# A two-block transformer kernel: attention probabilities of the second block turned by the vector engine and by small DMAs

## The chip, the cores and the metric

The kernel runs on one core of a Trainium2 chip. TensorE (PE in the rows) multiplies matrices, with its weight loads shown apart as PEld; VectorE (DVE) and ScalarE (ACT) work on elements; GpSimd (POOL) does a few masks; SyncE (SP) issues most DMAs. The metric is the device time of one execution in microseconds (us), as the median over runs.

## The reference

A sequence of 512 tokens of width 1024 passes two blocks in float32. The change lies in the second one. What is computed around it, cut to the core:

```python
h = rms_norm_2(x, norm_g)
proj = h @ w_in                      # u, g_rnn, q, k, v, g_attn, m_rnn, m_attn
u = causal_depthwise_conv_2(u, conv_w, conv_b)
y_rnn = rg_lru(u, ...) * silu(g_rnn)
# sliding window attention: 16 query heads, 4 key/value heads, blocks of 128 queries,
# keys of the block before and of the own block, one sink per head
scores = einsum("bnqkgd,bnjkd->bnkgqj", qb, kw) / sqrt(64)
scores = where(valid, scores, -inf)
m = maximum(max(scores, -1), sink)
p = exp(scores - m)
probs = p / (sum(p, -1) + exp(sink - m))
out = einsum("bnkgqj,bnjkd->bnqkgd", probs, vw)
y_attn = rope'd attention out * silu(g_attn)
merged = sigmoid(m_rnn) * (y_rnn @ w_rnn_out) + sigmoid(m_attn) * (y_attn @ w_attn_out)
x = x + merged @ w_o
```

The probabilities come with queries on the partitions; the product with the values needs keys on the partitions, so each 128x128 square of probabilities has to be transposed.

## The kernel before

**Weights.** All weights lie in DRAM as 216 chunks of 128x1024 float32, eight 128x128 tiles each, in the order of use. `w_load` (L153) brings a chunk into one of two `raw` buffers through SP's queue. `w_split` makes two fp32r halves of it: ACT casts the high half `wh` (L169), DVE subtracts for the low half `wl` (L170). There are three buffers of each. `take` walks through the chunks: at the first tile of chunk c it splits c to c+2 and loads up to c+4. A load waits until the split two chunks earlier has freed its buffer, and a cast until TensorE has finished with a chunk three earlier.

**Projections.** `project` multiplies activations by eight tiles, three matmuls of 128x512 for each (L293 to L295: high by high, high by low, low by high). Its weights are the stationary operand's stream, so one chunk is 24 matmuls. After every fourth tile it calls `tick`.

**Background work.** Attention runs in pieces between the matmuls of the projections. A unit is a Python generator; `yield cost, delay` ends a piece, takes its cost from a credit that each tick raises by `rate`, and holds the unit for `delay` ticks. Two units of lane "a" are open at a time. `finish` runs what is left of a unit without ticks. On top of this order of writing, a scheduler sets the final order of each engine by its own estimate of when data are ready; each engine then works strictly in that order. So instructions of one unit can stand late in one engine's row and early in another's.

**The second attention.** `window_attention(kvp, n)` (L940) is one unit: one pair of key/value heads, one block of 128 queries; there are 8 units, called unit 1 to 8 below (kvp 0 with n 0 to 3, then kvp 1). For each e of the pair it makes the scores of four query heads into PSUM (L955, L956), masks them into a 128x512 tile `p` (L960 for n = 0, else an ACT copy L962 and a DVE copy under a mask L963), takes the maximum (L965), exponentials with sums (L972) and normalises (L978). Then TensorE transposes the four squares into a PSUM bank by a matmul with the identity (L986, 8 a unit, 64 in all). ACT copies the bank to SBUF as `own` (L987), DVE multiplies it by a mask as `prev` for n > 0 (L990; 12 in all). Four matmuls (two for n = 0) make the output (L1000) and DVE multiplies it by the gate (L1004).

**What runs beside it.** After units 1 to 4 are queued, the gate projections run, then for m = 0 to 8 the recurrent branch (`lru`, convolution, scan), then `br` 0 (yr: the recurrent output, split for TensorE by L286 on ACT and L289 on DVE, times `w_rnn_out_2`), then `br` 1, which needs all units (`finish(*units)`, L1087) and splits `ya` in the same way.

Of the kernel before, what the change touches and what calls it, by code (L numbers as in the profile page):

```python
# [14 lines left out]
P = 128  # L15
# [111 lines left out]
def tile_hybrid_two_block(ctx, tc, xT, wts, prm_d, row_d, sgw_d, rope_d, sink_d, out):  # L127
    nc = tc.nc
# [49 lines left out]
    def take(n, width=P):  # L178

        res = []  # L180
        for _ in range(n * P // width):
            c, o = divmod(wpos[0], CH)
            if o == 0 or not res:
                for cc in range(c, c + 3):
                    w_split(cc)
                for cc in range(c, c + 5):
                    w_load(cc)
            h, l = conv[c]
            res.append((h[:, o * P : o * P + width], l[:, o * P : o * P + width]))
            wpos[0] += width // P  # L190
        return res

    lanes, clk = {"a": [], "b": []}, {"t": 0, "credit": 0.0, "rate": 1.0, "a": 2, "b": 1}

    def add_bg(gen, lane="a"):
        task = [gen, 0, lane]
# [55 lines left out]
    class Area:  # L254
# [10 lines left out]
        def tmp(self, dt=F32):  # L265
            return self.tile([P, T], dt)
# [673 lines left out]
    def window_attention(kvp, n):  # L940
        nk = P if n == 0 else 2 * P
        qs = slice(n * P, (n + 1) * P)
        ks = slice((n + 1) * P - nk, (n + 1) * P)
        prs = []
        for e in range(2):
            kv = 2 * kvp + e
            S4 = area[0].tile([P, 4, P], F32, "p")
            prs.append(S4)
            m4, nm4, es, sm = (area[0].tile([P, 4], F32, "s") for _ in range(4))
            per = T // nk  # L950
            for j0 in range(0, 4, per):
                ps = bank("aux")
                for d in range(per):
                    z, q = ps[:, d * nk : (d + 1) * nk], QS[kv][:, j0 + d, qs]
                    PE.matmul(z, lhsT=q, rhs=KS[kvp][:, 2 * e, ks], start=True, stop=False)  # L955
                    PE.matmul(z, lhsT=q, rhs=KS[kvp][:, 2 * e + 1, ks], start=False, stop=True)  # L956
                z = ps.rearrange("p (d k) -> p d k", d=per)
                x = S4[:, j0 : j0 + per]
                if n == 0:
                    V.tensor_tensor(out=x, in0=z, in1=mask[:, 0:1].to_broadcast([P, 4, P]), op=ALU.add)  # L960
                else:
                    A.copy(out=x, in_=z[:, :, P:nk])  # L962
                    V.copy_predicated(x, mask[:, 1:2].bitcast(mybir.dt.int32).to_broadcast([P, 2, P]), z[:, :, 0:P])  # L963
                yield 0.5, 0
            V.tensor_reduce(out=m4, in_=S4, axis=mybir.AxisListType.X, op=ALU.max)  # L965
            sk = sink[:, kv * 4 : kv * 4 + 4]
            V.scalar_tensor_tensor(out=m4, in0=m4, scalar=0.125, in1=sk, op0=ALU.mult, op1=ALU.max)
            V.tensor_scalar(out=nm4, in0=m4, scalar1=-1.0, scalar2=None, op0=ALU.mult)  # L968
            V.tensor_tensor(out=es, in0=sk, in1=m4, op=ALU.subtract)
            A.activation(es, es, AF.Exp)  # L970
            for j in range(4):
                A.activation(  # L972
                    S4[:, j], S4[:, j], AF.Exp, scale=0.125, bias=nm4[:, j : j + 1], accum_out=sm[:, j : j + 1]
                )
            yield 0.95, 1
            V.tensor_tensor(out=sm, in0=sm, in1=es, op=ALU.add)
            V.reciprocal(out=sm, in_=sm)
            V.tensor_tensor(out=S4, in0=S4, in1=sm.unsqueeze(2).to_broadcast([P, 4, P]), op=ALU.mult)  # L978
            yield 0.9, e


        own, prev = [tmp(), tmp()], []
        for e in range(2):
            ps = bank("aux")
            for j in range(4):
                PE.transpose(ps[:, j * P : (j + 1) * P], prs[e][:, j], ident)  # L986
            A.copy(out=own[e], in_=ps)  # L987
            if n > 0:
                prev.append(tmp())
                V.tensor_tensor(  # L990
                    out=prev[e].rearrange("p (a b) -> p a b", a=4), in0=ps.rearrange("p (a b) -> p a b", a=4),
                    in1=mask[:, 2:3].to_broadcast([P, 4, P]), op=ALU.mult,
                )
        yield 1.4 if n else 0.1, 2
        po = bank("aux")
        sums = [(VV[:, n], own)] + ([(VD[:, n - 1], prev)] if n else [])
        for i, (v, w) in enumerate(sums):
            for e in range(2):
                f = kvp * P + e * 64
                PE.matmul(  # L1000
                    po[e * 64 : e * 64 + 64], lhsT=v[:, f : f + 64], rhs=w[e], start=i == 0, stop=i == len(sums) - 1
                )
        y = ya[kvp][:, :, qs]
        V.scalar_tensor_tensor(  # L1004
            out=y, in0=po.rearrange("p (a b) -> p a b", a=4), scalar=0.5, in1=y, op0=ALU.mult, op1=ALU.mult
        )
        yield 0.66, 5
# [11 lines left out]
            high_low(f, lo, hi, QS[2 * kvp][:, j])  # L1019
            high_low(f, hi, lo, QS[2 * kvp + 1][:, j])  # L1020
    finish(norm_task)
    clk.update(rate=1.05)
    units = []
    for kvp in range(2):
        ya.append(grp(F32))
# [176 lines left out]
```

## Time and profile before

| what | us |
|---|---|
| median of 3 runs | 1285.73 (1285.55 to 1285.8) |
| profiled execution, its own time | 1285.55 |
| its span, first to last instruction | 1283.8 |
| TensorE busy | 1272.5 |
| VectorE busy | 870.3 |
| ScalarE busy | 599.4 |

The span is what the profile shows of an execution; 1.75 us of the profiled execution lie outside it. Busy time is the time in which an engine has at least one instruction in work. Matmuls overlap: a 128x512 matmul lasts 390 ns in the rows, and the next starts some 227 ns after it, so the cost of a matmul in a row of matmuls is the distance of two starts, not its length. The same holds for DVE and ACT on a smaller scale. The granted TensorE clock is 0.998 of full speed over the whole span, which is the 2.4 GHz level.

### The profile page before, as it was taken

Reading aid. Unit: us, or ns where it says so; the run is one execution under the profiler, and the core shown is the slowest. Engines: PE = TensorE matmul, PEld = TensorE weight load, DVE = VectorE, ACT = ScalarE, POOL = GpSimd, SP = SyncE. Lnnn points to the kernel's source line nnn. Section 1 sums busy time; section 2 is a strip of 40 time slices with the busy share of each in tenths; the row PEclk is TensorE's granted clock in tenths of the full one; section 3 lists DMA queues with packets and bytes.
Section 4 is the critical chain, followed back from the end, with each engine's and each line's share of the span. In section 5 each row is a group of like instructions: output and inputs, shape, how many; then the busy total and the mean of one; then the engine's idle time right before and its main releaser. Section 6 shows DMA issues by size and latency. Waiting matters only on the chain.

```text
span 1283.8 us, 15409 instructions
## 1 busy us (share of the span) xinstructions
PE 1272.5 (99%) x5890; PEld 1033.8 (81%) x5890; DVE 870.3 (68%) x1313; ACT 599.4 (47%) x964; POOL 45.8 (4%) x85
## 2 busy tenths in 40 slices
PE   9999999999999999999999999999999999999997
PEld 7888787778788888888888888888878777788886
DVE  6899998776447697666664333897678896633355
ACT  6733555546323464444443222554558875532232
POOL 0100004320000000000000000000000000000000
PEclk9999999999999999999999999999999999999999
DMA  6332322112333423333333333324222222223341
GB/s 212 131 99 83 99 83 82 60 56 83 99 107 120 134 77 106 98 99 99 99 99 103 116 109 110 105 84 130 69 84 96 81 82 66 82 83 99 132 131 66
DMA packets 39114, 126.80 MB, mean 99 GB/s; under 512 B 4480, under 2 KB 6656, under 8 KB 39040
## 3 DMA queue, kind: packets, MB, share of 16 engines
q1 hardware_dynamic: 37808, 124.76, 30.7%
q8 instruction: 46, 0.75, 0.2%
q10 hardware_dynamic: 1232, 1.05, 0.2%
q14 instruction: 28, 0.23, 0.1%
HBM read 121.60 MB, written 4.19 MB: 98 GB/s over the span
## 4 chain that ended last, share of the span: by engine, by line
PE 95%; DVE 3%; ACT 1%; issue 1%; POOL 0%; DVEq 0%; ACTq 0%
PE mm L293 29%; PE mm L294 29%; PE mm L295 29%; PE aux L1000 1%; PE aux L638 1%; PE aux L293 1%; PE aux L295 1%; PE aux L294 1%; PE aux L669 1%; PE aux L986 1%; PE aux L955 1%; PE aux L682 1%; PE aux L956 1%; DVE t L1137 0%; PE aux L520 0%
## 5 line engine op out<-in xcount | busy, mean ns | idle before, releaser
L293 PE MATMUL mm<-g,wh 128*128 128x512 f32 x1592 | 623.7, 392 | 0.0
L294 PE MATMUL mm<-g,wh 128*128 128x512 f32 x1592 | 620.9, 390 | 0.4 <-DVE g L289 0.4
L295 PE MATMUL mm<-g,wl 128*128 128x512 f32 x1592 | 620.7, 390 | 0.0
L170 DVE TENSOR_TENSOR wl<-raw,wh 128x1024 fp32r<-128x1024 f32 (+1 forms) x212 | 258.1, 1218 | 212.8 <-ACT wh L169 210.0
L169 ACT CAST wh<-raw 128x1024 fp32r<-128x1024 f32 (+1 forms) x211 | 221.5, 1050 | 370.0 <-PE mm L294 267.2
L293 PEld LDWEIGHTS mm<-g,wh 128*128 128x128 f32 x1592 | 299.0, 188 | 67.0 <-issue 5.3
L295 PEld LDWEIGHTS mm<-g,wl 128*128 128x128 f32 x1592 | 299.0, 188 | 62.9 <-issue 0.3
L294 PEld LDWEIGHTS mm<-g,wh 128*128 128x128 f32 x1592 | 299.1, 188 | 61.5 <-DVE g L289 1.1
L490 DVE SCALAR_TENSOR_TENSOR g<-g,prm,g 128x505 f32<-128x505 f32 (+28 forms) x120 | 82.6, 742 | 0.8
L286 ACT CAST g<-t 128x512 fp32r<-128x512 f32 x46 | 28.1, 620 | 64.8 <-DVE t L822 54.3
L809 DVE SCALAR_TENSOR_TENSOR t<-mm,prm,t 128x511 f32<-128x511 f32 x72 | 53.7, 746 | 1.3
L289 DVE TENSOR_TENSOR g<-t,g 128x512 fp32r<-128x512 f32 x46 | 31.8, 698 | 14.3 <-ACT g L286 14.1
L286 ACT CAST g<-g 128x512 fp32r<-128x512 f32 x44 | 25.9, 619 | 23.7 <-DVE g L760 14.2
L972 ACT ACTIVATE p<-p,s 128x128 f32<-128x128 f32 x64 | 24.9, 390 | 19.1 <-DVE s L968 19.1
L820 ACT ACTIVATE t<-t 128x512 f32<-128x512 f32 x22 | 13.9, 632 | 40.4 <-DVE t L809 40.4
L656 DVE TENSOR_TENSOR_SCAN t<-t,zero 128x512 f32<-128x512 f32 (+3 forms) x32 | 27.1, 850 | 7.5 <-POOL t L651 7.3
L289 DVE TENSOR_TENSOR g<-g,g 128x512 fp32r<-128x512 f32 x44 | 29.2, 689 | 2.6 <-ACT g L286 2.1
L807 ACT ACTIVATE t<-mm,prm 128x512 f32<-128x512 f32 x36 | 27.9, 774 | 0.0
L376 ACT ACTIVATE t<-g 128x512 f32<-128x512 f32 (+1 forms) x29 | 17.1, 591 | 20.5 <-DVE g L1116 16.9
L356 ACT ACTIVATE g<-g,prm 128x512 fp32r<-128x512 f32 x24 | 17.2, 717 | 18.0 <-DVE g L768 16.9
L1098 DVE SCALAR_TENSOR_TENSOR t<-t,mm 128x512 f32<-128x512 f32 x8 | 5.5, 689 | 27.1 <-PE mm L295 27.1
L651 POOL TENSOR_SCALAR_AFFINE_SELECT t<-t 128x128 f32<-128x128 f32 x32 | 17.4, 544 | 146.1 <-ACT t L647 146.0
(265 smaller groups left out, 1205.0 us busy)
## 6 DMA issues: line engine op xcount, KB each, us to landing
raw<-in_wts SPq DMA_DIRECT2D x215, 512.0 KB, 3.6
g<-in_xT SPq DMA_DIRECT2D x8, 256.0 KB, 5.8
t<-in_xT SPq DMA_DIRECT2D x8, 256.0 KB, 3.7
spill<-g SPq DMA_DIRECT2D x8, 256.0 KB, 3.2
g<-spill SPq DMA_DIRECT2D x8, 256.0 KB, 4.1
out<-t ACTq DMA_DIRECT2D x4, 256.0 KB, 2.3
out<-t SPq DMA_DIRECT2D x4, 256.0 KB, 2.4
g<-in_row SPq DMA_DIRECT2D x1, 768.0 KB, 6.5
```

What stands on the lines that cost most here:

```text
L169: A.copy(out=h[:, o : o + step], in_=raw[c][:, o : o + step])
L170: V.tensor_tensor(out=l[:, o : o + step], in0=raw[c][:, o : o + step], in1=h[:, o : o + step].bitcast(F32), op=ALU.subtract,)
L286: A.copy(out=h, in_=src)
L289: V.tensor_tensor(out=l, in0=src, in1=h.bitcast(F32), op=ALU.subtract)
L293: PE.matmul(ps, lhsT=lh, rhs=rh, start=start, stop=False)
L294: PE.matmul(ps, lhsT=lh, rhs=rl, start=False, stop=False)
L295: PE.matmul(ps, lhsT=ll, rhs=rh, start=False, stop=stop)
L490: V.scalar_tensor_tensor(out=a[:, d:T], in0=c[:, 0 : T - d], scalar=pr("cv_w", (30 - d) * 4 + i), in1=a[:, d:T], op0=ALU.mult, op1=ALU.add,)
L656: V.tensor_tensor_scan(out=R[:, 0:cx][:, ::-1], data0=F[:, 0:cx][:, ::-1], data1=zero.to_broadcast([P, cx]), initial=1.0, op0=ALU.mult, op ...
L807: A.activation(a, y, AF.Identity, scale=pr("ffn_conv_w", 88 + m), bias=pr("ffn_conv_b", m))
L809: V.scalar_tensor_tensor(out=a[:, d:T], in0=y[:, 0 : T - d], scalar=pr("ffn_conv_w", (2 - d) * 44 + m), in1=a[:, d:T], op0=ALU.mult, op1=A ...
L972: A.activation(S4[:, j], S4[:, j], AF.Exp, scale=0.125, bias=nm4[:, j : j + 1], accum_out=sm[:, j : j + 1])
```

## The change

The four squares are no longer transposed on TensorE. DVE turns each 32x32 square of `p` in place of position (STREAM_TRANSPOSE, 128x512, one an e, 16 in all), into a tile `turned`. The squares then have to change places: ACT copies the four diagonal squares' strips into the new tile `w` (32 partitions by 4x32 each, 64 copies in all), and the twelve others go by DMA from SBUF to SBUF on SP's queue (32 partitions, 4 runs of 32 elements each: 16 KB a DMA, 192 DMAs in all), issued three at a time by `move()`. `prev` is now made from `w` in SBUF. For n = 0, where there is no `prev`, DVE copies 128x4 elements of `w` onto themselves. The order of the two halves of the output's sum is reversed, delays and costs of the yields change, and from the second block's gate projections on, `take` loads up to c+3 instead of c+4.

```diff
-                for cc in range(c, c + 5):
+                for cc in range(c, c + clk["ahead"]):
                     w_load(cc)
...
+        own, moves = [], []
+        cuts = [slice(32 * i, 32 * i + 32) for i in range(4)]
+        def move():
+            for o, i in moves.pop(0) if moves else ():
+                nc.sync.dma_start(out=o, in_=i)
...
-                yield 0.5, 0
+                move()
+                yield 0.5, 1
...
+            move()
             yield 0.95, 1
...
-            yield 0.9, e
-        own, prev = [tmp(), tmp()], []
+            yield 0.7, 0
+            turned, w = tmp(), tmp()
+            V.transpose(out=turned, in_=S4.rearrange("p a b -> p (a b)"))
+            own.append(w)
+            src, dst = (x.rearrange("p (a b) -> p a b", a=4) for x in (turned, w))
+            for i in range(4):
+                r = slice(32 * i, 32 * i + 32)
+                A.copy(out=dst[r, :, r], in_=src[r, :, r])
+                moves.append([(dst[c, :, r], src[r, :, c]) for c in cuts if c != r])
+            yield 0.7, 0
+        while moves:
+            move()
+            yield 0, 1
+        prev = []
         for e in range(2):
-            ps = bank("aux")
-            for j in range(4):
-                PE.transpose(ps[:, j * P : (j + 1) * P], prs[e][:, j], ident)
-            A.copy(out=own[e], in_=ps)
+            w = own[e].rearrange("p (a b) -> p a b", a=4)
             if n > 0:
                 prev.append(tmp())
                 V.tensor_tensor(
-                    out=prev[e]..., in0=ps..., in1=mask[:, 2:3].to_broadcast([P, 4, P]), op=ALU.mult,
+                    out=prev[e]..., in0=w, in1=mask[:, 2:3].to_broadcast([P, 4, P]), op=ALU.mult,
                 )
+            else:
+                w = w[:, 0, 0:P:32]
+                V.tensor_copy(out=w, in_=w)
-        yield 1.4 if n else 0.1, 2
+        yield 1.4 if n else 0.1, 1
...
-        sums = [(VV[:, n], own)] + ([(VD[:, n - 1], prev)] if n else [])
+        sums = ([(VD[:, n - 1], prev)] if n else []) + [(VV[:, n], own)]
...
-    clk.update(rate=1.05)
+    clk.update(rate=1.05, ahead=4)
```

The changed kernel's lines are some 20 higher; L1021 there is L1000 here, L1008 is L990, L1025 is L1004, L1117 is L1096, L961 and L962 are L955 and L956, and L990 is the new transpose of DVE.

**Place A: the end of the recurrent branch, DVE.** The kernel before, the last of the four DVE splits of yr's second half (`g_8198`), which TensorE's first product of `br` 0 waits for:

```order
L1054 SCALAR_TENSOR_TENSOR t_8179<-t_8179,t_8175 128x512
L965 TENSOR_REDUCE s_8236<-p_8235 128x4
L1056 TENSOR_TENSOR g_7255<-g_7255,t_8179 128x512
L967 SCALAR_TENSOR_TENSOR s_8236<-s_8236,sink_6301 128x4
L990 TENSOR_TENSOR t_8306<-aux_8300,mask_6303 128x512
L968 TENSOR_SCALAR s_8237<-s_8236 128x4
L969 TENSOR_TENSOR s_8238<-sink_6301,s_8236 128x4
L170 TENSOR_TENSOR wl_8356<-raw_8221,wh_8355 128x1024
L289 TENSOR_TENSOR g_8198<-g_7255,g_8196 128x512
```

The changed kernel, the same place (`g_8251` is the split):

```order
L170 TENSOR_TENSOR wl_8271<-raw_8147,wh_8270 128x1024
L1074 TENSOR_TENSOR t_8228<-t_8228,t_8227 128x512
L289 TENSOR_TENSOR g_8251<-g_7265,g_8249 128x512
L1075 SCALAR_TENSOR_TENSOR t_8232<-t_8232,t_8228 128x512
L969 COPY_PREDICATED p_8316<-mask_6303,aux_8321 128x256
L1077 TENSOR_TENSOR g_7265<-g_7265,t_8232 128x512
L1008 TENSOR_TENSOR t_8351<-t_7789,mask_6303 128x512
L1008 TENSOR_TENSOR t_8353<-t_8050,mask_6303 128x512
L289 TENSOR_TENSOR g_8251<-g_7265,g_8249 128x512
```

The two products `prev` of unit 3 now stand ahead of the last split. From the last convolution's first step (`u_8133`, L1088) to that split DVE has 44 instructions.

**Place B: units 7 and 8, TensorE.** In the kernel before, unit 8's last rows on TensorE stand between the gate projections of `br` 0's end (`mm_8985`), with a full chunk and more of other matmuls behind them before `br` 1 begins:

```order
L986 MATMUL aux_8955<-ident,p_8838 128x128 x4
...
L986 MATMUL aux_8963<-ident,p_8890 128x128 x4
...
L1000 MATMUL aux_9004<-t_8953,v_6184 64x512
L1000 MATMUL aux_9004<-t_8954,v_6184 64x512
L1000 MATMUL aux_9004<-t_8961,vd_6388 64x512
L1000 MATMUL aux_9004<-t_8969,vd_6388 64x512
```

In the changed kernel the outputs of unit 7 (`aux_9198`) and unit 8 (`aux_9308`) stand among the first matmuls of `br` 1 (`mm_9339` is its first gate projection), and unit 8's scores (`aux_9209` to `aux_9257`) come between the parts of unit 7's output:

```order
L1021 MATMUL aux_9198<-t_9194,vd_6388 64x512
L961 MATMUL aux_9209<-g_6391,g_6500 128x256
...
L295 MATMUL mm_9339<-g_6380,wl_9085 128x512
L1021 MATMUL aux_9198<-t_9196,vd_6388 64x512
L1021 MATMUL aux_9198<-t_9060,v_6184 64x512
L1021 MATMUL aux_9198<-t_9160,v_6184 64x512
...
L1021 MATMUL aux_9308<-t_9304,vd_6388 64x512
...
L1021 MATMUL aux_9308<-t_9306,vd_6388 64x512
```

The last units have moved down behind the point at which `br` 1 is opened.

**Place C: units 7 and 8, DVE and SP.** What stands before `prev` of unit 7's second e (`t_9196`) on DVE in the changed kernel, from its transpose on:

```order
L990 STREAM_TRANSPOSE t_9159<-p_9066 128x512
L170 TENSOR_TENSOR wl_9139<-raw_9088,wh_9138 128x1024
L1008 TENSOR_TENSOR t_9194<-t_9060,mask_6303 128x512
L1117 SCALAR_TENSOR_TENSOR g_8247<-t_8724,mm_8779 128x512
...
L289 TENSOR_TENSOR g_9316<-g_6846,g_9314 128x512 x2
L969 COPY_PREDICATED p_9204<-mask_6303,aux_9209 128x256
...
L974 SCALAR_TENSOR_TENSOR s_9205<-s_9205,sink_6301 128x4
```

and SP's row there, where the 48 moves of the two units stand between the weight loads:

```order
L153 DMA raw_9142<-in_wts 128x1024
L950 DMA t_9060<-t_9059 32x4x32 x12
L950 DMA t_9160<-t_9159 32x4x32 x12
L153 DMA raw_9344<-in_wts 128x1024
L153 DMA raw_9376<-in_wts 128x1024
L950 DMA t_9236<-t_9235 32x4x32 x12
L950 DMA t_9283<-t_9282 32x4x32 x12
L153 DMA raw_9412<-in_wts 128x1024
```

SP's row of before has only weight loads there, one behind the other; in the changed one each move waits for its transpose, and the loads behind it wait with it.

## Rows read from the trace of the kernel before

**Rows 1.** The page's head: busy time of each engine with its share of the span, and the chain that ended last, by engine.

```profile
PE 1272.5 (99%) x5890; PEld 1033.8 (81%) x5890; DVE 870.3 (68%) x1313; ACT 599.4 (47%) x964; POOL 45.8 (4%) x85
PE 95%; DVE 3%; ACT 1%; issue 1%; POOL 0%; DVEq 0%; ACTq 0%
```

**Rows 2.** The timeline of TensorE (start in us, length in us, instruction) around three of the 14 runs of transposes: the first, the one with the longest wait, and the last. A bracket is idle time before the instruction and what ended it.

```profile
909.38 0.39 PE L295 MATMUL mm<-g,wl 128*128 128x512 f32 x1
909.61 1.32 PE L986 MATMUL aux<-ident,p 128*128 128x128 f32 x8
910.69 0.48 PE L293 MATMUL mm<-g,wh 128*128 128x512 f32 x1
911.00 0.40 PE L294 MATMUL mm<-g,wh 128*128 128x512 f32 x1
...
1058.40 0.40 PE L294 MATMUL mm<-g,wh 128*128 128x512 f32 x1
1059.71 0.63 PE L986 MATMUL aux<-ident,p 128*128 128x128 f32 x4 [0.91 <-DVE p L978]
...
1060.41 0.39 PE L293 MATMUL mm<-g,wh 128*128 128x512 f32 x1
...
1117.01 0.39 PE L294 MATMUL mm<-g,wh 128*128 128x512 f32 x1
...
1117.98 0.39 PE L293 MATMUL mm<-g,wh 128*128 128x512 f32 x1
```

**Rows 3.** All transposes of TensorE, from the view of the line L986: count; shortest, median and longest in ns; first and last start in us.

```profile
L986 PE MATMUL aux<-ident,p x64: 270/273/302, 909.6 to 1117.6; 128*128 128x128 f32 x64
```

**Rows 4.** Busy time in the stretch of place A, 1021 to 1049 us, and in the stretch of all eight units, 890 to 1125 us: the length, then PE, PEld, DVE, ACT and POOL (busy us, number of instructions), the granted clock, the DMA engines' mean busy share and GB/s.

```profile
1021.00:1049.00 28.00, 27.62 (x126) 22.33 (x125) 27.59 (x44) 24.45 (x41) 0.00 (x0) 1.00 0.23 73
...
890.00:1125.00 235.00, 233.38 (x1101) 183.96 (x1100) 175.16 (x316) 150.80 (x325) 0.00 (x0) 1.00 0.26 81
```

**Rows 5.** Place A. First, from the view of its line, ACT's step that starts the last convolution. Then the timeline of DVE at the beginning, in the middle and at the end of the stretch, and TensorE's first product with the low half that DVE made last.

```profile
L1065 ACT ACTIVATE u<-mm,prm x1: 772/772/772, 1020.3 to 1020.3; 128x512 f32<-128x512 f32 x1
...
1021.08 2.32 DVE L1067 SCALAR_TENSOR_TENSOR u<-mm,prm,u 128x511 f32<-128x511 f32 x3 [0.84 <-ACT u L1065]
...
1029.76 0.69 DVE L1045 SCALAR_TENSOR_TENSOR t<-t,u 128x512 f32<-128x512 f32 x1
1030.36 0.68 DVE L289 TENSOR_TENSOR g<-g,g 128x512 fp32r<-128x512 f32 x1
...
1041.56 1.22 DVE L170 TENSOR_TENSOR wl<-raw,wh 128x1024 fp32r<-128x1024 f32 x1
1042.69 0.69 DVE L1053 TENSOR_TENSOR t<-t,t 128x512 f32<-128x512 f32 x1
...
1048.35 0.68 DVE L289 TENSOR_TENSOR g<-g,g 128x512 fp32r<-128x512 f32 x1
...
1049.26 0.39 PE L294 MATMUL mm<-g,wh 128*128 128x512 f32 x1
1049.49 0.40 PE L295 MATMUL mm<-g,wl 128*128 128x512 f32 x1
```

**Rows 6.** The timeline of TensorE in the middle of a group of scores.

```profile
1009.58 0.28 PE L956 MATMUL aux<-g,g 128*128 128x256 f32 x1
1009.69 0.28 PE L955 MATMUL aux<-g,g 128*128 128x256 f32 x1
```

**Rows 7.** Groups of DVE and ACT instructions by line: count, then busy us, mean ns of one, then idle time before them and what ended it. The scan is from 1020 to 1050 us, the others from 890 to 1130 us.

```profile
L1054 DVE TENSOR_TENSOR_SCAN t<-t,t 128x512 f32<-128x512 f32 x3 | 3.7, 1221 | 0.0
...
L978 DVE TENSOR_TENSOR p<-p,s 128x512 f32<-128x512 f32 x16 | 11.0, 688 | 0.4
L965 DVE TENSOR_REDUCE s<-p 128x4 f32<-128x512 f32 x16 | 10.9, 682 | 0.3
L963 DVE COPY_PREDICATED p<-mask,aux 128x256 f32<-128x256 int32 x24 | 10.4, 443 | 2.1 <-ACT p L962 1.9
L976 DVE TENSOR_TENSOR s<-s,s 128x4 f32<-128x4 f32 x16 | 2.6, 162 | 14.7 <-ACT p L972 14.7
L990 DVE TENSOR_TENSOR t<-aux,mask 128x512 f32<-128x512 f32 x12 | 8.1, 683 | 1.1 <-ACT t L987 1.1
...
L169 ACT CAST wh<-raw 128x1024 fp32r<-128x1024 f32 x36 | 37.7, 1046 | 29.8 <-PE mm L294 18.3 <-issue 9.8 <-ACT t L987 1.0
L972 ACT ACTIVATE p<-p,s 128x128 f32<-128x128 f32 x64 | 24.9, 390 | 19.1 <-DVE s L968 19.1
L987 ACT COPY t<-aux 128x512 f32<-128x512 f32 x16 | 9.2, 580 | 5.4 <-PE aux L986 5.3
```

**Rows 8.** Of the whole span, from the view of its line: ACT's copy of 128x128 elements out of PSUM, in the first attention.

```profile
L647 ACT ACTIVATE t<-aux 128x128 f32<-128x128 f32 x8 | 2.4, 311 | 0.0
```

**Rows 9.** DMAs: SP's issue of a weight load (ns, shortest, median, longest); from the page, KB and median us from issue to landing of the outputs and of the table `sink` (64 bytes a partition); the landing of the eight spills out of SBUF (256 KB each); and what SP's weight loads waited for between 880 and 1130 us (us, times, longest).

```profile
L153 SPq DMA_DIRECT2D raw<-in_wts x215: 327/328/432, 2.7 to 1240.4; - x108
...
out<-t SPq DMA_DIRECT2D x4, 256.0 KB, 2.4
...
sink<-in_sink SPq DMA_DIRECT2D x1, 8.0 KB, 3.5
...
DMA to landing us min/median/max: 2.0/3.2/4.5
...
SPq L153 <- DVE wl L170: 205.1, 36, 9.8
```

More of the change, by code (lines that the diff above doesn't have):

```diff
@@ L191, in take @@
         return res
-    lanes, clk = {"a": [], "b": []}, {"t": 0, "credit": 0.0, "rate": 1.0, "a": 2, "b": 1}
+    lanes, clk = {"a": [], "b": []}, {"t": 0, "credit": 0.0, "rate": 1.0, "a": 2, "b": 1, "ahead": 5}
     def add_bg(gen, lane="a"):
@@ L943, in window_attention @@
         ks = slice((n + 1) * P - nk, (n + 1) * P)
-        prs = []
+        own, moves = [], []
[3 more added lines that the diff above has]
+                nc.sync.dma_start(out=o, in_=i)
         for e in range(2):
@@ L947, in window_attention @@
             S4 = area[0].tile([P, 4, P], F32, "p")
-            prs.append(S4)
             m4, nm4, es, sm = (area[0].tile([P, 4], F32, "s") for _ in range(4))
@@ L990, in window_attention @@
                 V.tensor_tensor(
-                    out=prev[e].rearrange("p (a b) -> p a b", a=4), in0=ps.rearrange("p (a b) -> p a b", a=4),
+                    out=prev[e].rearrange("p (a b) -> p a b", a=4), in0=w,
                     in1=mask[:, 2:3].to_broadcast([P, 4, P]), op=ALU.mult,
                 )
-        yield 1.4 if n else 0.1, 2
+            else:
+                w = w[:, 0, 0:P:32]
+                V.tensor_copy(out=w, in_=w)
+        yield 1.4 if n else 0.1, 1
         po = bank("aux")
-        sums = [(VV[:, n], own)] + ([(VD[:, n - 1], prev)] if n else [])
+        sums = ([(VD[:, n - 1], prev)] if n else []) + [(VV[:, n], own)]
         for i, (v, w) in enumerate(sums):
```

## Prediction

> **What bounds the kernel now.** I read the head of the page first, then the chain, then TensorE's timeline around the removed instructions, then DVE at the place where TensorE waits closest behind it, then the DMA views. TensorE is busy 99% of the span and makes 95% of the chain [rows 1]. So TensorE time that is removed is worth all of itself, provided that TensorE does not have to stand and wait instead; what the other engines gain or lose counts only where it makes TensorE wait. DVE has slack on the average (68%), but not everywhere: in the 28 us of place A it is busy 27.59 [rows 4].
>
> **What is removed on TensorE.** A transpose lasts 273 ns in the rows [rows 3], but four of them together take 0.63 from the first start to the last end [rows 2], so their starts are (0.63 - 0.27) / 3 = 0.12 apart. I use the distance of starts, not the length: 64 x 0.12 = 7.7 us. A run also costs an edge: the first matmul behind it reads 0.48 instead of 0.39 and its successor starts 0.31 later, not 0.23. The whole cost of a run is the start of the second matmul behind it, less the start of the last matmul before it, less two usual distances of 0.23 [rows 5]. For the first run 911.00 - 909.38 - 0.46 = 1.16; for the one with the longest wait 1060.41 - 1058.40 - 0.46 = 1.55, of which 0.91 is a wait for DVE's normalising; for the last 1117.98 - 1117.01 - 0.46 = 0.51 [rows 2]. Over all 14 runs, of which these are the first, the dearest and the last, the same subtraction gives 10.0 us: 7.7 of work, the rest edges and waits. ACT also loses 16 copies of 0.58 [rows 7], which TensorE does not feel.
>
> The Trainium skill speaks against the change here: "VectorE: DVE Perf Modes", sections "The three transpose paths" and "Rules for kernel authors", gives a 128x128 transpose to TensorE where the result may land in PSUM, and says that DVE turns only 32x32 blocks, which is why the DMAs are there. Its table has 390 ns for one (bf16), by which 64 would be worth 25 us; the trace has 0.12 us from start to start, and the trace decides: less is to be had than the table suggests.
>
> **What is added, and what it costs at the three places where TensorE can feel it.** No row shows DVE's 32x32 transpose. Bounds from the nearest rows: below, a copy under a mask of half as many elements, 0.44; above, a scan of as many, 1.22. I take 0.6 from start to start like other 128x512 instructions, since `p`'s normalising reads and writes the same shape [rows 5, 7]. No row shows a DMA from SBUF to SBUF in runs of 128 bytes. Issue: 0.33 (median) to 0.43 (longest) of a weight load; I take 0.33. Landing: 2.0 (fastest spill) to 3.5 (`sink`, 64 bytes a partition); I take 2.4, the outputs' median, since they too start in SBUF [rows 9]. ACT's 64 strip copies take 0.31 at most, like a copy of four times the elements [rows 8]: 20 us in place of the 9.3 removed, in a stretch where ACT is busy 150.80 of 235.00 us [rows 4]; I count 0.75 of it, four copies of 0.19, where a unit waits for them (unit 8). `prev` costs the same from SBUF as from PSUM in my sum (0.68 [rows 7], bounds 0.6 to 0.75, no matter for the total). The copies of 128x4 for n = 0 are 0.16 each like a 128x4 addition [rows 7], hidden.
>
> *Place A.* Before, DVE worked without a gap from 1021.08 to 1049.03 and TensorE took the last low half at 1049.26 [rows 5]: the two just met. In the changed order TensorE has, from the last convolution's product to that point, 99 matmuls x 0.228 = 22.6, 12 score matmuls x 0.12 = 1.4 [rows 6] and one output matmul 0.24: 24.3 us. DVE's path to it is ACT's step 0.77 and a handing over of 0.08, then 44 instructions: three steps of the convolution 2.3 (the 2.32 of the row), three scans and two splits of weights at 1.14 (41.56 to 42.69) 5.7, two `tensor_scalar` at 0.4, two predicated copies at 0.36, a reduce 0.66, five small ones 0.8, and 26 others at 0.60 (29.76 to 30.36) 15.6 [rows 5, 7]: 26.5. Together 27.4, so TensorE waits 3.1 us. DVE has one transpose and one `prev` more there and two splits of weights less, but TensorE has less other work to fill with. Bounds: 0, if TensorE comes to this point later than its order's count says, to 4, with a transpose at 1.22 and slower handing over.
>
> *Unit 7's second `prev`* (t_9196). From unit 7's last scores TensorE has 45 matmuls, 16 scores and one output matmul: 10.3 + 1.9 + 0.2 = 12.4. The data need a copy and mask 1.0, reduce 0.66, three small 0.5, exponentials with the sink's one 1.85 (0.39 each [rows 7]), two small 0.4, normalising 0.6, transpose 0.6, a split of weights 1.14, t_9194 0.6, four gate products 2.4, three splits of ya 1.8, three predicated copies 1.05, a reduce 0.6 and t_9196 0.7: 13.9. So 1.5 us of wait. The twelve moves (12 x 0.33 + 2.4 = 6.4) lie beside 7.6 us of DVE work between transpose and `prev` and are hidden; at 0.43 and 3.5 they are 8.7 and add 1.1.
>
> *Unit 8's second `prev`* (t_9306). Here nothing hides them. TensorE has 3 output matmuls, 64 matmuls and one more output matmul behind t_9196: 15.6. The data: 9.5 of softmax, transpose, splits and the diagonal copies' 0.75, then 12 x 0.33 + 2.4 = 6.4 of moves, then `prev` 0.65: 16.55. That is 0.95 of wait. Then the gate 0.65 and ACT's cast 0.55 stand before a product for which 5 matmuls (1.14) are left with the output's own time, which makes 0.3 more: 1.25 together. At 0.43 and 3.5 the moves add 2.3.
>
> *Loads one chunk later.* Worth nothing by itself: SP's loads waited 205.1 us in 36 waits for DVE's split to free the buffer [rows 9], and casts waited for TensorE, 18.3 us, not for a landing [rows 7]. What hides it is that weights are split well ahead of their use. SP's row now holds moves between loads; twelve of them hold a load back by 4 us, twenty-four by 8. If the cover were gone, one landing would show, some 3.5 us by `sink`'s. The 192 moves carry 24,576 runs of 128 bytes, 3.1 MB in all, on DMA engines that are busy 0.26 of the stretch [rows 4].
>
> **The sum.** 10.0 removed, 3.1 + 1.5 + 1.25 = 5.85 of new waits: 4.15 us gained. The profiled execution took 1285.55 (span 1283.8 and 1.75 outside), so 1281.4; the median of the runs is 0.18 higher, and I put the forecast there: 1281.6. Unknown ends: transposes at 1.22 cost 0.6 more at A, 0.6 at unit 7 and 1.2 at unit 8 (+2.4); slow moves +3.4; without place A's wait -3.1, without any -5.85.
>
> **Rivals.** *The waits mostly do not come.* For it: units have two in flight, the scheduler puts other products in between, and TensorE was busy 233.38 of 235.00 us over the whole stretch before [rows 4]; against: the order is fixed and place A's count has no slack. If all but 0.8 of the 5.85 goes: 1276.5.
>
> *The moves are slow.* Landing 4.5, as the slowest spill did [rows 9], and issue 0.43: 12 x 0.43 + 4.5 = 9.7 instead of 6.4, so unit 7 pays 9.7 - 7.6 = 2.1 and unit 8 3.3 more. The waits are 5.85 + 5.4 = 11.25 against 10.0 removed: 1287.0, no change. For it: runs of 128 bytes, which no row shows; against: the bytes are few. The Trainium skill, "DMA: Bandwidth & Descriptors", section "Specifications", says that transfers under 512 bytes fall below line rate because they read, modify and write; no run so far shows that here, and by it this rival gains.
>
> *DVE stands behind the moves* (the other side). DVE works in order; `prev` of a unit waits for twelve DMAs, and splits of weights queue behind it, without which TensorE has nothing at all to multiply. Likewise SP's row puts two sets of moves ahead of a load. Its place is units 7 and 8. The price is what a set of twelve takes beyond 7.6 us at unit 7 and beyond 6.4 at unit 8, and it outweighs the gain of 4.15 from a set of about 9 us on. With landings of 7 us and an issue of 0.43 a set takes 12.2: 4.6 + 5.8 = 10.4 more than forecast, 1292.0. For it: splits stand behind `prev` there; against: a landing of 7 us occurs nowhere in these rows.
>
> *The change does not do what it says:* the shorter lookahead moves no weight in time, as reckoned above; this is part of the forecast and has no time of its own.
>
> **How the numbers follow.** Forecast 0.48, its own range 1278.5 to 1284; few waits 0.20; slow moves 0.20; DVE behind the moves 0.12. A difference of 0.2%, 2.6 us, is what a measurement of this kernel can tell: faster is below 1283.2, slower above 1288.3. Of the forecast's 0.48, 0.40 lie below 1283.2 and 0.08 above; with the first rival faster has 0.60. Slow moves give 0.17 to the same and 0.03 to slower: same 0.25, and slower 0.15 with the last rival. The range reaches from the first rival, 1276.0, to the upper end of slow moves, 1288.5, and leaves out the last rival and little else.
>
> **What would show it.** TensorE's busy time down by about 7 us and the group of L986 gone; DVE's transpose between 0.6 and 0.7; a move 0.33 to issue and 2 to 3 to land; TensorE idle about 3 us before the low product of yr (ended by DVE's split L289) and 1 to 1.5 before the outputs of units 7 and 8 (ended by `prev`). It is wrong if a move takes over 4 us to land, if DVE stands idle for DMAs with a split of weights behind it, or if TensorE waits for L170 or for casts.

## The result, and the profile after

The changed kernel takes 1294.95 us (median of 4 runs, 1294.89 to 1295.92) against 1285.72 before: a ratio of 1.0072, interval 1.006 to 1.0084. It is slower by 9.2 us where 4.1 us of gain were forecast. The profiled execution took 1295.92, with a span of 1294.2.

The page's head, to be read beside [rows 1]: busy time of each engine, then the chain that ended last.

```profile
PE 1273.5 (98%) x5826; PEld 1030.0 (80%) x5826; DVE 880.2 (68%) x1333; ACT 610.7 (47%) x1012; POOL 47.1 (4%) x85
PE 91%; DVE 4%; SPq 2%; ACT 2%; issue 1%; DMA 0%; POOL 0%; DVEq 0%; ACTq 0%
```

The 64 transposes are gone (x5890 became x5826), but TensorE's busy time did not fall, and its share of the chain did: SP's queue is now 2% of it. The waits of TensorE from 880 us on (us, times, longest):

```profile
PE aux L1021 <- DVE t L1008: 7.5, 3, 5.2
PE mm L293 <- ACT t L1114: 1.6, 1, 1.6
PE mm L293 <- ACT g L286: 1.1, 1, 1.1
...
PE mm L293 <- ACT wh L169: 0.4, 1, 0.4
PE mm L294 <- DVE g L289: 0.3, 1, 0.3
PE mm L295 <- DVE wl L170: 0.2, 1, 0.2
```

What the new operations cost, from the views of their lines (ns: shortest, median, longest) and, of ACT's strip copies, from the page (count, busy, mean):

```profile
L990 DVE STREAM_TRANSPOSE t<-p x16: 699/704/715, 904.0 to 1150.6; 128x512 f32<-128x512 f32 x16
...
L950 SPq DMA_DIRECT2D t<-t x192: 585/599/1864, 904.8 to 1161.1; - x192
...
DMA to landing us min/median/max: 1.8/1.8/5.0
...
L995 ACT COPY t<-t 32x128 f32<-32x128 f32 x64 | 18.9, 295 | 16.0 <-DVE t L990 15.5
```

The transpose costs what was taken: 0.70 long, and the next instruction starts 0.62 behind it (1120.83 to 1121.45). A strip copy costs what was given as its bound, 0.30, so four take 1.2 and not the 0.75 that was counted. A move lands sooner than taken (1.8) and is issued far more slowly: 0.60 an issue, 0.64 from start to start, where the dearest weight load was 0.43 [rows 9]. SP's row at units 7 and 8 (start, length, instructions):

```profile
1121.61 16.34 SPq L950 DMA_DIRECT2D t<-t  x24
1138.05 6.93 SPq L153 DMA_DIRECT2D raw<-in_wts  x2
1146.23 15.44 SPq L950 DMA_DIRECT2D t<-t  x24
1161.76 1.01 SPq L153 DMA_DIRECT2D raw<-in_wts  x2
```

Both sets of a unit stand in one row: 24 moves take 15.4 us. At unit 8 TensorE's timeline, with the output matmuls on L1021, and then DVE's transpose of the second head and the `prev` that ends TensorE's wait, read:

```profile
1156.01 1.04 PE L1021 MATMUL aux<-t,vd 128*64 128x512 f32 x2 [0.80 <-DVE t L1008]
1156.99 0.50 PE L293 MATMUL mm<-g,wh 128*128 128x512 f32 x1
...
1158.48 0.39 PE L293 MATMUL mm<-g,wh 128*128 128x512 f32 x1
1164.04 1.12 PE L1021 MATMUL aux<-t,vd 128*64 128x512 f32 x1 [5.17 <-DVE t L1008]
...
1167.64 0.79 PE L294 MATMUL mm<-g,wh 128*128 128x512 f32 x1
1168.23 0.63 PE L295 MATMUL mm<-g,wl 128*128 128x512 f32 x1
1168.66 0.63 PE L293 MATMUL mm<-g,wh 128*128 128x512 f32 x1
...
1150.64 0.71 DVE L990 STREAM_TRANSPOSE t<-p 128x512 f32<-128x512 f32 x1
...
1163.29 0.69 DVE L1008 TENSOR_TENSOR t<-t,mask 128x512 f32<-128x512 f32 x1 [6.29 <-DMA t<-t]
```

Behind the wait matmuls start 0.43 apart instead of 0.23. The granted clock tells why: the same columns as [rows 4], with the clock third from the end.

```profile
1160.00:1164.00 4.00, 0.00 (x0) 0.00 (x0) 0.69 (x1) 0.00 (x0) 0.00 (x0) 0.89 0.25 52
1164.00:1168.00 4.00, 3.96 (x7) 1.40 (x8) 0.25 (x1) 0.00 (x0) 0.00 (x0) 0.50 0.56 226
```

After a standstill of 5 us TensorE runs at 0.50, its 1.2 GHz level. Slow matmuls count as busy, and so does what the output products cost beyond before (both below), which is why busy time did not fall with the transposes. At place A there are four short waits in a row, and the same afterwards:

```profile
1034.52 0.50 PE L293 MATMUL mm<-g,wh 128*128 128x512 f32 x1 [1.07 <-ACT g L286]
1035.46 0.50 PE L293 MATMUL mm<-g,wh 128*128 128x512 f32 x1 [0.45 <-ACT wh L169]
...
1036.53 0.53 PE L294 MATMUL mm<-g,wh 128*128 128x512 f32 x1 [0.34 <-DVE g L289]
...
1037.67 0.79 PE L295 MATMUL mm<-g,wl 128*128 128x512 f32 x1 [0.18 <-DVE wl L170]
1038.26 0.63 PE L293 MATMUL mm<-g,wh 128*128 128x512 f32 x1
1038.69 0.63 PE L294 MATMUL mm<-g,wh 128*128 128x512 f32 x1
```

A wait is measured here as the distance of TensorE's two starts around it, less their usual distance, so it comes out longer than the idle time in the bracket. The loss place by place: place A 3.0 of waits and 1.3 of slow matmuls; at 1125.6 a wait of 1.7 that was not foreseen; unit 7 1.75; unit 8 0.96 (first head) + 5.33 (second head) of waits and, worked out with run e9 below, 2.9 of slow matmuls. These are 16.9. Another 2.9 are in the output products themselves, beside the clock (runs e13 to e18 below); a product is one call of `PE.matmul` for the output, two instructions in the rows. 19.8 less the 10.0 that the transposes cost makes 9.8; the profiled execution is 10.4 longer than that of before, and 1.0 longer than the other three of its kernel.

### The profile page after: what moved, and what is told of

It is laid out like the page before. It is cut to its first block, busy times and chain, and to the rows that moved or that the text cites. A ratio compares the mean times of both kernels' runs of the same rounds, so it can differ in the third digit from the quotient of the medians.

```text
span 1294.2 us, 15670 instructions
## 1 busy us (share of the span) xinstructions
PE 1273.5 (98%) x5826; PEld 1030.0 (80%) x5826; DVE 880.2 (68%) x1333; ACT 610.7 (47%) x1012; POOL 47.1 (4%) x85
## 4 chain that ended last, share of the span: by engine, by line
PE 91%; DVE 4%; SPq 2%; ACT 2%; issue 1%; DMA 0%; POOL 0%; DVEq 0%; ACTq 0%
PE mm L293 28%; PE mm L294 28%; PE mm L295 28%; SPq L950 2%; PE aux L1021 1%; PE aux L638 1%; DVE wl L170 1%; PE aux L293 1%; PE aux L295 1%; PE aux L294 1%; PE aux L669 1%; PE aux L682 1%; DVE u L1088 0%; PE aux L961 0%; ACT p L979 0%
## 5 line engine op out<-in xcount | busy, mean ns | idle before, releaser
L170 DVE TENSOR_TENSOR wl<-raw,wh 128x1024 fp32r<-128x1024 f32 (+1 forms) x212 | 257.7, 1216 | 193.0 <-ACT wh L169 192.3
L169 ACT CAST wh<-raw 128x1024 fp32r<-128x1024 f32 (+1 forms) x211 | 221.5, 1050 | 348.5 <-PE mm L294 255.0
L289 DVE TENSOR_TENSOR g<-t,g 128x512 fp32r<-128x512 f32 x46 | 31.7, 696 | 14.3 <-ACT g L286 14.2
L995 ACT COPY t<-t 32x128 f32<-32x128 f32 x64 | 18.9, 295 | 16.0 <-DVE t L990 15.5
L356 ACT ACTIVATE g<-g,prm 128x512 fp32r<-128x512 f32 x24 | 17.2, 717 | 17.9 <-DVE g L768 16.9
```

Source lines behind the costliest of these rows:

```text
L169: A.copy(out=h[:, o : o + step], in_=raw[c][:, o : o + step])
L170: V.tensor_tensor(out=l[:, o : o + step], in0=raw[c][:, o : o + step], in1=h[:, o : o + step].bitcast(F32), op=ALU.subtract,)
L289: V.tensor_tensor(out=l, in0=src, in1=h.bitcast(F32), op=ALU.subtract)
```

## The experiments

Theories: Q, SP's issue of moves makes the waits of units 7 and 8; D, DVE's and ACT's own order makes them; L, the later loads do; K, a standstill also costs the clock behind it. Each run has its own kernels of before beside it (1285.6 to 1286.0).

**e1: loads one chunk earlier again.**

```diff
-    clk.update(rate=1.05, ahead=4)
+    clk.update(rate=1.05)
```

> The changed kernel with the weight loads issued one chunk earlier again (up to c+4). Theory Q (TensorE waits for units 7 and 8 because SP issues 24 moves in a row at 0.64 us each): no difference to the changed kernel, 1295 within 2 us, with SP again issuing sets of 24 and unit 8's wait of 5 us still there. Theory L (the later loads are what starves TensorE): 1286 or less.

Measured 1295.82 (ratio 1.008, 1.0064 to 1.0097). Unit 8's wait is 5.2 as before. The lookahead is worth nothing either way; L falls.

**e2: no moves.** One copy by ACT in place of strips and DMAs.

```diff
-            for i in range(4):
...
-                A.copy(out=dst[r, :, r], in_=src[r, :, r])
-                moves.append([(dst[c, :, r], src[r, :, c]) for c in cuts if c != r])
+            A.copy(out=w, in_=turned)
```

> Leaves out the exchange of the squares: ACT copies the turned tile whole into w (one copy of 128x512 an e), and no DMA moves anything, so the probabilities stay wrongly placed. Theory Q: the waits of units 7 and 8 (1.75 + 0.96 + 5.3 us) and the slow clock behind them (about 3.5 us) go, place A's 3 us stay: 1283 to 1286. Theory D (DVE's and ACT's own order is late, the moves lie beside it): 1292 or more.

1280.44 (0.9957, 0.9942 to 0.9972), even below the range: place A and 1125 lost their waits too. The moves, their strips or their steps cost 14.5 us. D as stated (1292 or more) falls, but this run removes the empty steps as well and so changes the order; e12 below keeps them.

**e3: every second move from GpSimd's queue.**

```diff
-            for o, i in moves.pop(0) if moves else ():
-                nc.sync.dma_start(out=o, in_=i)
+            for j, (o, i) in enumerate(moves.pop(0) if moves else ()):
+                (nc.sync if (j + len(moves)) % 2 else G).dma_start(out=o, in_=i)
```

> Every second move is issued from GpSimd's queue, which does nothing in this stretch, the others from SP's. Theory Q: the 24 moves before unit 8's output take half the time on SP if GpSimd issues as fast, so the wait of 5.3 us and the clock behind it go: 1285 to 1289. If GpSimd's issue or landing is slower than 1.3 us a move, nothing is won: 1293 to 1300. Theory D: 1293 to 1296 in either case.

1285.38 (0.9996, 0.9987 to 1.0005): Q holds. The issue of 96 moves on each queue, by the view of the line:

```profile
L950 SPq DMA_DIRECT2D t<-t x96: 585/599/1233, 904.8 to 1151.2; - x96
L950 POOL DMA_DIRECT2D t<-t x96: 551/551/683, 905.6 to 1150.5; - x96
```

No output product waits over 0.3 us; place A and 1125 wait as in the changed kernel.

**e4: units 7 and 8 transposed by TensorE.** `own` takes `S4`, and the loop of before (four `PE.transpose`, `A.copy`) is put back for `kvp == 1 and n > 1`.

> Units 7 and 8 transpose on TensorE as before (16 of the 64 transposes), units 1 to 6 as in the changed kernel. Theory Q: the waits of units 7 and 8 and the clock behind them go (11.5 us), 16 transposes with their edges come back (2.5 us): 1285 to 1287. Theory D: the waits move to other places, 1291 or more.

1285.58 (0.9999, 0.999 to 1.0008): 9.4 us go when units 7 and 8 alone are taken back, as Q has it.

**e5 and e9: needless matmuls in unit 8's wait**, 24 and then 6, behind the first product with the first head's `prev`:

```diff
+                if kvp == 1 and n == 3 and i == 0 and e == 0:
+                    fb = bank("aux")
+                    for _ in range(6):
+                        PE.matmul(fb[0:64], lhsT=v[:, f : f + 64], rhs=w[e], start=True, stop=True)
```

> The changed kernel with 24 needless matmuls (64x512 out, about 0.23 us each, 5.5 us) in the wait before the second product of unit 8's output; they need only what has already landed, and write a bank that nobody reads. Theory K (the wait itself stays, but the granted clock behind it no longer falls, so that the six output products and the next matmuls run at full speed): about 3 us faster than the changed kernel, 1291 to 1293, granted clock near 1.0 at 1164 to 1172. Without K: 1294 to 1297, since useless work can only cost.

> As the run with 24 needless matmuls, with 6: that run showed that one takes two instructions of 0.42, so 6 take 5.0 us and fit into unit 8's wait of 5.2. Theory K: the granted clock stays at 1.0 behind the wait, and the six output products and the next matmuls lose the 2.5 to 3.5 us that they now take longer: 1291 to 1293. Without K: 1294 to 1296.

e5 took 1306.27 (1.0158, 1.014 to 1.0176). My size was wrong: one such matmul is two instructions, 0.43 apart, so 24 took 20 us and ran past the end of the wait. e9 took 1294.12 (1.0063, 1.0046 to 1.0079). Its timeline and clock there:

```profile
1163.89 0.64 PE L1021 MATMUL aux<-t,vd 128*64 128x512 f32 x1 [1.84 <-DVE t L1008]
...
1165.77 0.50 PE L293 MATMUL mm<-g,wh 128*128 128x512 f32 x1
...
1164.00:1168.00 4.00, 4.00 (x16) 2.27 (x17) 1.44 (x3) 1.40 (x3) 0.00 (x0) 1.00 0.48 197
```

The wait ends at the same time (1163.89 against 1164.04), the clock stays at 1.00, and the six output instructions take 1.88 instead of 3.60. With the following matmuls of the changed kernel, eight distances in 3.01 instead of 1.82, the clock cost 2.9 us at unit 8. K holds in the rows. The time gained only 0.8, and by itself it lies in the range without K: the needless matmuls pushed seven useful ones (1.6 us), which the changed kernel does between the first product and the wait, out behind the wait.

**e6: each move cut in two** (two heads each, 384 DMAs).

> Each move is cut into two DMAs of two heads (64 runs of 128 bytes instead of 128; 384 DMAs, the same bytes). If SP's 0.60 of an issue is a price per DMA, a set of 24 becomes 48 and takes about 31 us instead of 15.5: 1310 or more. If it is a price per run, an issue takes about 0.3 and the time stays: 1294 to 1298.

1354.59 (1.0534, 1.0517 to 1.0551). An issue of half as many runs costs the same, so the price is one per DMA:

```profile
L951 SPq DMA_DIRECT2D t<-t x384: 585/594/1650, 904.7 to 1220.6; - x192
```

**e7 and e8: GpSimd copies the diagonal strips** (`G.tensor_copy` for `A.copy`), e8 with e3's two queues as well.

> GpSimd instead of ACT copies the 64 diagonal strips, all moves stay on SP. Theory A (ACT's strip copies, which stand in its row and wait for transposes with casts and tanh behind them, make the waits at place A, 3.0 us, and at 1125, 1.7 us): these go with their slow clock, 1288 to 1291. Theory S (the order in which softmax and transposes of units 3 and 4 stand on DVE there makes them): place A stays, 1292 to 1296.

> GpSimd copies the diagonal strips and issues every second move; SP issues the others. The sum of the last two: theory Q with A 1279 to 1282, as fast as without any moves; Q with S 1284 to 1287, as in the run with half the moves on GpSimd's queue.

e7: 1294.88 (1.0071, 1.0055 to 1.0087). Place A's waits shrink from 3.0 to about 1.9 us and its slow matmuls go, 1125 stays at 1.7, and the time is that of the changed kernel. Output products (19.3 in all against 18.6) and waits for `prev` (8.0 against 7.5) became longer and take a part of it back. A falls for 1125 and is at most a part of place A. e8: 1290.99 (1.0043, 1.0027 to 1.0059), slower than e3 against both expectations. Units 7 and 8 wait 2.5 us each again; GpSimd's row now holds four copies before every six of its moves. Whether that or the order made these waits was not taken apart.

**e10 and e11: a move as one run of 512 bytes.** The transpose writes, and the strips, moves and products read, tiles ordered by square first (`"p (i a x)"`), with SP alone and with two queues. The elements come out in other places than the reference's.

> The turned tile and w are laid out so that a move is 32 partitions of one run of 512 bytes instead of four of 128 bytes; 192 moves, the same bytes, all on SP's queue. Theory R (the issue price hangs on the shape of the access, one row a partition being as cheap as a weight load's 0.33): a set of 24 takes 9 us instead of 15.5, unit 8's wait and its slow clock go, 1286 to 1289. Theory P (a move within SBUF costs SP 0.6 whatever its shape): 1294 to 1296.

> The same layout, every second move on GpSimd's queue. By theory Q the moves are hidden already in the run with half the moves on GpSimd's queue (1285.4), and what remains is place A (3 us and its clock) and the wait at 1125 (1.7): 1284 to 1286 under R and under P alike; below 1283 only if the moves' time also delayed DVE's row at place A.

e10: 1293.16 (1.006, 1.0046 to 1.0075), e11: 1285.56 (0.9996, 0.9987 to 1.0005).

```profile
L950 SPq DMA_DIRECT2D t<-t x192: 507/588/1556, 904.6 to 1159.6; - x192
...
DMA to landing us min/median/max: 1.7/1.8/4.7
```

Issue 0.588 and landing 1.8: runs of 128 bytes make neither (on GpSimd's queue in e11 an issue took 0.498 instead of 0.551, a tenth less). Theory P, with unit 8 waiting 5.0; why an issue within SBUF is dearer than one of before stays open.

**e12: no moves, but the same steps** (e2 with `moves += [[] for _ in range(4)]`).

> As the run without moves (the exchange of the squares left out, one whole copy by ACT), but with the same list of empty steps, so that the unit's yields and ticks, and with them the order in which everything is written, are those of the changed kernel. Theory S (place A's 3 us with its clock and the 1.7 at 1125 come from where the steps put the softmax and the transposes on DVE and ACT): they come back, 1284 to 1287. Theory M (moves and strip copies themselves make them): as the run without moves, 1280 to 1281.5.

1282.5 (0.9969, 0.9958 to 0.9979), between the two expectations. Its waits decide:

```profile
PE mm L293 <- ACT t L1112: 1.6, 1, 1.6
PE mm L293 <- ACT g L286: 1.0, 1, 1.0
```

Without a single DMA, the waits of place A (1.15 + 0.72 + 0.50 + 0.57 by distances of starts) and of 1125 (1.75) are those of the changed kernel. S holds: they come from where the new yields put softmax and transposes. No `prev` makes TensorE wait any more, with every step in its place: this is what takes D away. But e12 has 4.7 us more of waits and slow matmuls than e2 (6.0 against 1.3) and is only 2.1 us slower, so something else was cheaper in it.

**e13 to e15: all moves at once, without steps**: on two queues; the same with units 7 and 8 on TensorE; on GpSimd's queue alone.

```diff
+                for j, c in enumerate(c for c in cuts if c != r):
+                    (nc.sync if (i + j) % 2 else G).dma_start(out=dst[c, :, r], in_=src[r, :, c])
```

> All 24 moves of a unit are issued right behind their strip copies, without steps of their own, half from SP's and half from GpSimd's queue. Theory S: the units run through as in the run without moves, place A and 1125 lose their waits, and with two queues units 7 and 8 wait little: 1279.5 to 1283, faster than both kernels. Theory M: 1284 to 1287.

> As the run before, with units 7 and 8 transposed by TensorE (2.5 us of transposes back, no move near the end). If units 7 and 8 still wait for moves there, this is the faster of the two: 1281 to 1283; if not, it is 1 to 2.5 us slower than it.

> All moves at once, all from GpSimd's queue at 0.55 an issue, none on SP's. Theory Q: what counts is the length of a set before unit 8's output, 24 x 0.55 = 13 us on one queue against 7.5 on two; so 2 to 5 us slower than with two queues, and still faster than the changed kernel, whose loads also wait behind the moves. If it equals two queues, unit 8 has slack by the new order.

1290.66 (1.0039, 1.0026 to 1.0052), 1287.47 (1.0013, 1.0004 to 1.0022) and 1293.1 (1.0056, 1.0042 to 1.0069). The first two miss all their ranges; e15 is 2.4 slower than e13, as Q has it. In e13 place A and 1125 have no wait, and TensorE waits 3.5 us in all, yet it is slower than e3. The reason stands in the timeline of its output products, here unit 8's:

```profile
1141.44 0.39 PE L295 MATMUL mm<-g,wl 128*128 128x512 f32 x1
1141.81 1.04 PE L1022 MATMUL aux<-t,vd 128*64 128x512 f32 x2
1142.78 0.50 PE L293 MATMUL mm<-g,wh 128*128 128x512 f32 x1
```

One product alone (two instructions) takes 0.97 from its start to the next matmul's. In the kernel before, the four of a unit stand together and take 1.87, 0.47 each:

```profile
938.47 1.08 PE L1000 MATMUL aux<-t,v 128*64 128x512 f32 x4
939.38 1.03 PE L1000 MATMUL aux<-t,vd 128*64 128x512 f32 x4
940.34 0.51 PE L293 MATMUL mm<-g,wh 128*128 128x512 f32 x1
```

**e16 to e18: the products put together** in e3, e13 and e14:

```diff
-            for e in range(2):
+            for e in (1, 0):
```

> Half the moves on GpSimd's queue, as in the third run, and the two heads' products of a unit's output in the order e = 1, 0, so that the first one needs what lands last and the four products of a unit follow each other without other matmuls between. Theory B (a product that stands alone takes 1.0, as long as two in a row, because neighbours write different halves of the partitions and overlap): the outputs' time falls from 16.8 to about 14 and nothing else changes: 1282 to 1284, faster than the kernel before. Without B: 1285 to 1287.

> All moves at once on two queues, with the products in the order e = 1, 0. Theory B: the outputs' time falls from 22.0 to about 14, place A and 1125 have no wait in this order: 1282 to 1284; if the waits for the second head's squares grow instead, because the first product now waits for them too, 1285 to 1288.

> As the run before, with units 7 and 8 transposed by TensorE. Theory B: the outputs' time falls from 19.1 to about 14: 1281.5 to 1283.5; else 1286 to 1288.

1282.8 (0.9975, 0.9966 to 0.9984), 1281.87 (0.997, 0.9958 to 0.9981) and 1282.33 (0.9972, 0.9961 to 0.9982): all three are faster than both kernels (0.25 to 0.3% under the one of before, with intervals below 1), and B holds in all three. Unit 8's products in e17:

```profile
1140.21 1.08 PE L1022 MATMUL aux<-t,vd 128*64 128x512 f32 x4 [1.03 <-DVE t L1009]
1141.09 1.06 PE L1022 MATMUL aux<-t,v 128*64 128x512 f32 x4
1142.08 0.50 PE L295 MATMUL mm<-g,wl 128*128 128x512 f32 x1
```

Four products take 1.87, two together 1.01, one alone 0.97 to 1.00. Summed from start to start over a kernel, the 28 products take 14.0 us before, 18.6 in the changed kernel (1.75 of its 4.7 more is unit 8's clock), 16.8 in e3, 22.0 in e13, and 13.4 and 13.6 in e16 and e17. From e13 to e17 that is 8.4 us of the 8.8 gained, from e3 to e16 it is 3.5, of which 0.7 more of waiting takes back a part: 2.6 gained. It also settles e12: its products take 14.6 us, those of e2 16.9.

## Why the prediction was wrong

**The saving (10.0) held, nearly.** The losses found in the trace are 19.8 and the profiled executions lie 10.4 apart, which leaves 9.4 for it. It was not measured by itself.

**Place A (3.1) held in size, not in what ends it.** TensorE waits 3.0 us, but more for ACT's casts (1.52 of the 2.04 idle in the brackets) than for DVE (0.52), and 1.3 of slow clock follow. DVE's last split, whose path the sum priced, ends none of the waits. That the size agrees is luck in part; that the new order makes the wait was right, and e12 shows it.

**Unit 7 (1.5) was 1.75.** The moves were not hidden as said, though: `prev` waited for a DMA for 1.81 us:

```profile
1139.36 0.69 DVE L1008 TENSOR_TENSOR t<-t,mask 128x512 f32<-128x512 f32 x1 [1.81 <-DMA t<-t]
```

The size came out right by another path, which is luck.

**Unit 8 (1.25) is the step that failed: "12 x 0.33 + 2.4 = 6.4 of moves".** The landing was better, 1.8. The issue was 0.64 from start to start, and the second set queued behind the first in one row of 24: when the second transpose ended (1151.35), about 4 moves of the first set were still to be issued (estimate, 5.1 us into the row at 0.64 each), and then came its own 12. So `prev` started 11.9 us behind the transpose (1163.29) and not 0.75 + 6.4 = 7.15, and TensorE waited 6.3 in place of 1.25. The prediction counted both sets for the weight load behind them, but one for `prev`. The upper bound of 0.43 from [rows 9] did not reach, because no row of before issues a DMA within SBUF. Half the moves on another queue (e3) takes 9.6 us away, no moves 14.5.

**Three terms were missing.** The clock behind a wait: 1.3 at place A and 2.9 at unit 8. The wait at 1125, 1.7, for a `tanh` behind exponentials on ACT. And "one output matmul 0.24": that is the distance of two instructions in a row of them, and a product has two, so it costs 0.47 in a row of four; standing alone, as the reversed sum and the early first `prev` left it at place A and at units 7 and 8, it costs 1.0, and the 28 cost 2.9 more than before. Unit 8's wait is 5.0 of what separates forecast and trace, the clock 4.2, the products 2.9 and 1125 1.7.

**The rivals.** "The moves are slow" had the right resource and the wrong term: slow to issue, not to land. "DVE stands behind the moves" had the right place, the right sign and nearly the time (1292), and 0.12. But no split of weights starved TensorE (0.2 us for L170): it waited for `prev` itself. "The waits mostly do not come" falls. That the shorter lookahead does nothing was right (e1). Of the prediction's own signs of being wrong, landing over 4 us came only as an exception (median 1.8, longest 5.0), but DVE did stand idle for DMAs, 14.3 us in five waits, one of them (3.8) with a split of weights behind it, and TensorE did wait for casts, at place A.

Landing took 1.8 us with runs of 128 bytes and with runs of 512 bytes (e10), so no run here shows the price of small runs that spoke for slow moves.

The Trainium skill, "DMA: Bandwidth & Descriptors", section "Issuing engines are not separate DMA queues", says that issuing from several engines saves only the sequencer's time, usually small beside the DMA. The runs agree on what is saved (e3, 9.6 us) and not that it is small here: a move took 0.60 of issue to 1.8 of landing, and 15.4 us of issue stood in one row.

## What to carry to other kernels

Count the DMAs that stand in one queue ahead of the datum, both sets and not one, and take their issue from a DMA of the same kind: where many small transfers are cut, a second issuing engine can be worth more than longer runs (here 9.6 us in e3 against 1.8 in e10). Price a wait of TensorE with the slow matmuls behind it, and look at which instructions it separates, since small matmuls that overlap in a row lose that when a scheduler pulls one forward. The change's idea was sound and its form was not: with two queues and the products together it gains 3 to 4 us.

## What the runs showed of the hardware that was not expected

- A DMA of 16 KB from SBUF to SBUF costs SP 0.60 us of issue with 128 runs of 128 bytes and 0.588 with 32 runs of 512 (e10); half of it, 64 runs of 128 bytes, costs 0.594 (e6). GpSimd's issue is 0.551 (e3), and 0.498 with runs of 512 (e11). Weight loads cost SP 0.33 in the changed kernel.
- A 64-row product of two instructions takes as long alone (0.97 to 1.00) as two such products into different halves of the partitions (1.01). The Trainium skill, "TensorEngine Tiling (Array Packing)", section "Key Properties", says that tiles of the array work independently and can run at the same time; the rows agree, with 0.43 between instructions on one half only (e5) and 0.23 on the average of eight where halves alternate (1.87).
- After 5.2 us without work the granted clock was 0.50, and stayed at 1.00 when needless matmuls filled most of the same wait (e9). Waits of 1.0 to 1.8 us elsewhere left no slow matmuls, nor did one of 2.54 in e8; another of 2.47 in e8, one of 2.56 in e15 and the four in a row at place A did.
